# A pooling mixer and gated ConvFFN layer on one core: the second norm's factors by DMA, the first averaging matrices by GpSimd's queue, another order of the first loads

## The chip, the cores and the metric

The kernel runs on one core of one Trainium2 chip. The metric is device time in microseconds (us) of one execution. Before the change, three runs gave 671.47, 671.95 and 671.97 us.

The engines named below are TensorE (PE in the profile; PEld is its weight load), VectorE (DVE), ScalarE (ACT), GpSimd (POOL) and SyncE (SP). SP and POOL each issue DMAs on a queue of their own (q1 and q0 in the profile); 16 DMA engines carry them out.

## The reference

x is 1024 tokens by 1024 channels, float32. With these sizes there is one layer, and its mixer is the pooling one:

```python
def rms_norm(x, g):
    y = x * lax.rsqrt(jnp.mean(x * x, axis=-1, keepdims=True) + EPS)
    return y * g

def pool_mixer(x, w, b, scale):        # windows 2, 4, 8, 16: one for each 256 channels
    ...
    groups.append(window_sum / count - xf[..., group])
    ...
    y = jnp.einsum('bsgc,gcd->bsgd', d, w).reshape(bsz, seq, D_MODEL) + b
    return scale * y

def conv_ffn(x, w_in, conv_w, conv_b, w_out):
    h = causal_depthwise_conv(x @ w_in, conv_w, conv_b)
    val, gate = jnp.split(h, 2, axis=-1)
    return (jax.nn.silu(gate) * val) @ w_out

h = rms_norm(x, norm_mix_g)
x = x + pool_mixer(h, pool_w, pool_b, pool_scale)
x = x + conv_ffn(rms_norm(x, norm_ffn_g), ffn_w_in, ffn_conv_w, ffn_conv_b, ffn_w_out)
```

The hidden width of the ConvFFN is 2 x 2816.

## The kernel before

**Stages.** x is cut into 8 tiles of 128 tokens. The mixer handles a tile at a time; its results, normed a second time and transposed, fill the operand n2f. Then come the product with w_in (1024 x 5632), the convolution and gate, and the product with w_out (2816 x 1024), both as seven products of half-size blocks in place of eight, in float32r parts (rows L402 and L761 of the profile). These two matrix stages take up nearly all of the span. The change touches the mixer only, which is the first 65 us.

**The mixer for tile j.** `rstd_of` (ScalarE squares a tile with a sum along its rows, takes a root; VectorE makes of it two factors whose product is 1/sqrt) gives the row factors. `mixer_norm` multiplies the averaging matrices (`band`, for tile 0 `band0`, which is a part of the constants `cst`) by them, so the norm is folded into the matrices. `windows` multiplies x by these matrices on TensorE (psd); tile 0's first columns are corrected with `fac`, the later tiles' first 16 tokens with `edges`, which come from the last 16 tokens of all tiles (`x_edge`, `edge_norm`, `mixer_edges`, ps_edges). ScalarE copies psd to dh. `mixer_out` multiplies dh by the scaled weights wps, adds the bias through the rows `bias_hl` and a matrix of ones (psy, L288 and L291), and VectorE adds x (x1). `mixer_out_stats` takes the statistics of x1 by `rstd_of`, `ffn_norm` makes n2 from x1, the row factor and `gains[0]`, the second norm's factors with one row in each of the 128 partitions, and `ffn_operand` transposes it (pst).

**Factors before.** `gain_rows` makes that tile of factors: the factors stand in `par_sb`, 8 to a partition (columns from GF); eight products on TensorE with `ident`, each with one column broadcast, spread them over all partitions, and ScalarE copies the result to `gain_b`, times FOLD (64). FOLD is a constant that is also in the averaging matrices.

**Order.** Each engine works its instructions in order. `issue_after` sets an instruction behind another on the same engine; the last part of the code shown lists the order of the mixer's first tiles by such marks. SP's queue is issued in this order: x0 in two halves; cst up to E0 (band0 and fac); x1; 16 columns of par_sb (from GM: first and second norm's factors); the rest of cst; pool_w in two; x2; x_edge; then, behind the bias rows, x3 to x7 and the convolution's factors in par_sb. POOL's queue loads only rows8 here (pool_scale and pool_b, in 8 partitions). POOL itself fills `idle`, `pick`, `bias_hl` and the four matrices of `band`. TensorE first multiplies `idle` seven times (`keep_warm`), then spreads pool_scale with `pick` (ps_scale).

**PSUM.** The mixer's banks (`bank2`) rotate over three double banks: idle_ps, psd0, ps_gain, psd1, psy0 and so on.

Of the kernel before, what the change touches and what calls it, by code (L numbers as in the profile page):

```python
# [7 lines left out]
F32 = mybir.dt.float32  # L8
F32R = mybir.dt.float32r
BF16 = mybir.dt.bfloat16  # L10
AF = mybir.ActivationFunctionType
ALU = mybir.AluOpType
PSUM = bass.MemoryType.PSUM

P = 128
S = 1024
D = 1024
F = 2816
NS = S // P
NK = D // P  # L20
NF = F // P
NG = 4
# [3 lines left out]
EPS = 1e-6  # L26

FOLD = 2 * D**0.5

CW, CB, GM = 0, 3 * 2 * NF, 4 * 2 * NF  # L30
GF = GM + NK
NPAR = GF + NK


FAC = NG * P // 2
E0 = FAC + 2 * NG * HALO
# [27 lines left out]
def trunk_kernel(ctx: ExitStack, tc: tile.TileContext, x, consts, par, rows, pool_w, w_in, w_out, out):  # L64
    nc = tc.nc

    const = ctx.enter_context(tc.tile_pool(name="const", bufs=1))
    dram = ctx.enter_context(tc.tile_pool(name="dram", bufs=1, space=bass.MemoryType.DRAM))
# [8 lines left out]
    pp = pre.enter_context(tc.tile_pool(name="pre", bufs=1))  # L77
    ps_p = pre.enter_context(tc.tile_pool(name="ps_p", bufs=3, space=PSUM))

    def bank2(name):  # L80
        return ps_p.tile([P, 2 * NH], F32, tag="ps", name=name)

    def raw_tile(name):
        return work.tile([P, 2, D], F32, tag="raw", name=name, bufs=2)
# [15 lines left out]
    def load_x(j):  # L100
        if j < 2 or j >= 2 + XBUFS:
            xs[j] = hls.tile([P, D], F32, tag="hl", name=f"x{j}", bufs=7)
        else:
            xs[j] = pp.tile([P, D], F32, tag="x", name=f"x{j}", bufs=XBUFS)
        for cols in HALVES if j == 0 else [slice(0, D)]:
            nc.sync.dma_start(xs[j][:, cols], x[j * P : (j + 1) * P, cols])

    cst = pp.tile([P, BD], F32, tag="cst", name="cst")
# [3 lines left out]
    def affine(t, src, op, fill, base, pattern, step):  # L112
        nc.gpsimd.affine_select(out=t, in_=src, compare_op=op, fill=fill, base=base, pattern=pattern, channel_multiplier=step)

    rows_raw = raw_tile("rows_raw")
    scale = rows_raw[:, 0, :GRP]
    rows8, bias8 = (rows_raw[:NK, 1, i * NH : i * NH + 2 * P].rearrange("k (r p) -> k r p", p=P) for i in range(2))
    bias8 = bias8.bitcast(F32R)
    idle = work.tile([P, NH], BF16, tag="sum", name="idle", bufs=3)
    nc.gpsimd.memset(idle, 0.0)  # L120
    nc.vector.memset(scale, 0.0)
    eps_t = const.tile([P, 1], F32, tag="eps", name="eps_t")
    nc.vector.memset(eps_t, D * EPS)
    warm = pp.tile([P, 1], F32, tag="warm", name="warm")
    with tc.issue_after(nc.scalar.dma_start(scale[:NG, :], rows[0].rearrange("(g d) -> g d", d=GRP)).ins):
        nc.scalar.activation(warm, eps_t, AF.Sqrt)

    nc.gpsimd.dma_start(rows8, rows.rearrange("r (k p) -> k r p", p=P))

    pick = pp.tile([P, NG], F32, tag="pick", name="pick")  # L130
    nc.gpsimd.memset(pick, 0.0)
    affine(pick, pick, ALU.not_equal, 1.0, 0, [[1, NG]], -1)
    bias_hl = pp.tile([P, D], F32R, tag="bias_hl", name="bias_hl")
    nc.gpsimd.memset(bias_hl.bitcast(F32), 0.0)
    for g, w in enumerate(WINDOWS):

        m = band[:, g, :]
        nc.gpsimd.memset(m, FOLD / w)
        affine(m, m, ALU.is_ge, 0.0, 0, [[1, P]], -1)
        affine(m, m, ALU.is_gt, 0.0, w, [[-1, P]], 1)  # L140
        affine(m, m, ALU.not_equal, FOLD / w - FOLD, 0, [[1, P]], -1)
    par_sb = const.tile([P, NPAR + PAD], F32, tag="par", name="par_sb")
    wp_raw = raw_tile("wp_raw").rearrange("p a (c d) -> p (a c) d", d=GRP)

# [5 lines left out]

    keep_warm(7)
    load_x(0)
    nc.sync.dma_start(cst[:, :E0], consts[:, :E0])
    load_x(1)
    nc.sync.dma_start(par_sb[:, GM:NPAR], par[:, GM:])
    nc.sync.dma_start(cst[:, E0:], consts[:, E0:])
    for g in range(0, NG, 2):
        nc.sync.dma_start(wp_raw[:, 2 * g : 2 * g + 4, :], pool_w[g : g + 2].rearrange("g (k p) d -> p (g k) d", p=P))
    load_x(2)
# [6 lines left out]
    ident = cst[:, ID:]  # L166

    marks = {}

    def rstd_of(src, name, halves=False):  # L170
        junk = pp.tile([P, D], BF16, tag="junk", name=f"junk_{name}")
        st = pp.tile([P, 8], F32, tag="st", name=f"st_{name}", bufs=8)
        part, first, ms, root, q, inv, half = (st[:, i : i + 1] for i in range(7))
        bias = eps_t
        if halves:
            bias = first
            nc.scalar.activation(junk[:, :NH], src[:, :NH], AF.Square, accum_out=half)
            nc.vector.tensor_scalar(first, half, D * EPS, None, op0=ALU.add)
            src, junk = src[:, NH:], junk[:, NH:]
        nc.scalar.activation(junk, src, AF.Square, accum_out=part)  # L180
        marks[name] = nc.scalar.activation(root, part, AF.Sqrt, bias=bias).ins
        nc.vector.tensor_scalar(ms, part, first if halves else D * EPS, None, op0=ALU.add)

        nc.vector.scalar_tensor_tensor(q, root, root, ms, op0=ALU.mult, op1=ALU.add)
        nc.vector.reciprocal(inv, q)
        return root, inv
# [6 lines left out]
    def edge_norm():  # L193
        marks["edge"] = normed(edge_band, band_e, rstd_of(x_edge, "e"))

    def mixer_norm(j):
        t = bands[j] = pp.tile([P, NG, P], F32, tag="bandr", name=f"bandr{j}", bufs=2)
        for groups in [slice(0, 2), slice(2, 4)] if j == 0 else [slice(0, NG)]:
            marks[f"band{j}"] = normed(t[:, groups, :], (band if j else band0)[:, groups, :], stats[j])
# [18 lines left out]
    wps = pp.tile([P, 2 * NG, GRP], F32, tag="wps", name="wps")  # L218
# [8 lines left out]
    def mixer_weights(scale_b, chunks):  # L227
        for c in chunks:
            marks["wps"] = nc.vector.scalar_tensor_tensor(
                wps[:, c, :], scale_b[c // 2], par_sb[:, GM + c : GM + c + 1], wp_raw[:, c, :], op0=ALU.mult, op1=ALU.mult  # L230
            ).ins
# [4 lines left out]
    def pool_bias():  # L236
        marks["bias"] = nc.scalar.activation(bias8[:, 0, :], b8, AF.Copy).ins
        marks["bias_dve"] = nc.vector.tensor_tensor(bias8[:, 1, :], b8, bias8[:, 0, :].bitcast(F32), ALU.subtract).ins
        for l in range(2):
            m = nc.sync.dma_start(bias_hl[l : l + 1, :].bitcast(F32), bias8[:, l, :].bitcast(F32)).ins  # L240
        with tc.issue_after(m):
            for j in range(3, NS):
                load_x(j)
            nc.sync.dma_start(par_sb[:, :GM], par[:, :GM])

    def gain_rows():
        ps = bank2("ps_gain")
        for k in range(NK):
            gain = par_sb[:, GF + k : GF + k + 1].to_broadcast([P, P])
            marks["gain_pe"] = nc.tensor.matmul(ps[:, k * P : (k + 1) * P], gain, ident, start=True, stop=True).ins  # L250
        gain_b = pp.tile([P, D], F32, tag="gain_b", name="gain_b")
        marks["gain"] = nc.scalar.activation(
            gain_b.rearrange("p (k s a) -> p k a s", k=NK, a=2), ps.rearrange("p (k a s) -> p k a s", k=NK, a=2), AF.Copy, scale=FOLD
        ).ins
        return gain_b

    ds, gains = {}, []

    def window_sums(j):
        ps = bank2(f"psd{j}")  # L260
# [19 lines left out]
    n2s = {}  # L280
# [16 lines left out]
            mixer_out_stats(j)  # L297

    def mixer_out_stats(j):
        n2s[j] = (n2s[j], rstd_of(n2s[j], f"b{j}"))  # L300

    def ffn_norm(j):
        x1, r = n2s[j]
# [179 lines left out]
    def stat(j):  # L483
        if j in xs and j not in stats:
            stats[j] = rstd_of(xs[j], f"a{j}", halves=j == 0)
# [13 lines left out]
    with tc.issue_after(marks["dh0"]), tc.issue_after(marks["wps"]):  # L499
        pool_bias()  # L500
    with tc.issue_after(marks["bias_dve"]):
        mixer_weights(scale_b, range(1, 2 * NG))
    with tc.issue_after(marks["psd0"]), tc.issue_after(marks["bias"]):
        gains.append(gain_rows())
    with tc.issue_after(marks["gain"]), tc.issue_after(marks["wps"]):
        stat(2)
        mixer_norm(2)
    with tc.issue_after(marks["gain_pe"]), tc.issue_after(marks["a2"]):
        mixer_window(1)
    with tc.issue_after(marks["dh1"]), tc.issue_after(marks["band2"]):  # L510
        edge_norm()
# [11 lines left out]
    with tc.issue_after(marks["dh1+"]), tc.issue_after(marks["edges"]):  # L523
        mixer_out_stats(0)
# [37 lines left out]
    halves = [slice(0, 2), slice(2, 4)]  # L562
# [28 lines left out]
    def take(name):  # L591
# [15 lines left out]
    src = {  # L607
        "A11": lambda f: g_dram[f][:, s0], "A21": lambda f: g_dram[f][:, s1],
        "A12": lambda f: g_dram[f + NP2][:, s0], "A22": lambda f: g_dram[f + NP2][:, s1],
        "B11": lambda f: w_out[f * P : (f + 1) * P, s0], "B12": lambda f: w_out[f * P : (f + 1) * P, s1],  # L610
        "B21": lambda f: w_out[(f + NP2) * P : (f + NP2 + 1) * P, s0],
        "B22": lambda f: w_out[(f + NP2) * P : (f + NP2 + 1) * P, s1],
    }
# [91 lines left out]
    for k in range(-SLOOK, len(oevents)):  # L705
        p, f = oevents[k + SLOOK] if k + SLOOK < len(oevents) else (None, 0)
# [8 lines left out]
        with tc.issue_after(lasts[-1]) if lasts else nullcontext():  # L715
# [12 lines left out]
            p, f = oevents[k]  # L728
# [9 lines left out]
        if f == 0 and opens:  # L738
            for i in range(4):
                tag = ("XXYY" if set_ == "X" else "YZZZ")[i]  # L740
# [15 lines left out]
        for i, g, c, bank in steps:  # L756
            a, b = oops[p, g]
            alone = opens and (p, i) != ("P4", 3)
            for m, (u, v) in enumerate(((0, 0), (0, 1), (1, 0))):
                first = g == (NP2 - TAIL if c.start else 0) and m == 0  # L760
                nc.tensor.matmul(  # L761
                    bank, a[:, u, i * P : (i + 1) * P], woven(b[:, v, :])[:, c.start // 2 : c.stop // 2, :],
                    start=opens and first, stop=g == NP2 - 1 and m == 2, skip_group_check=not alone,
# [83 lines left out]
```

## Time and profile before

| | us |
|---|---|
| median of three runs | 671.95 |
| the profiled execution | 671.79 |
| its span, first to last instruction | 670.1 |
| TensorE busy | 663.4 |
| VectorE busy | 568.6 |
| ScalarE busy | 339.4 |
| GpSimd busy | 47.6 |

The mean granted clock of TensorE is 0.999. Durations and places below are those of the profiled execution; a time in us counts from its first instruction. In the chain of waits a row is: start, length, what the end of the kernel waited for there. In the timeline a row is: start, busy time, engine, line, operation, output <- inputs, shape, count, and in brackets the idle time just before it with what ended it. "issue" is time with no wait that the profile shows. A table by stretch has the busy time of each engine with its count of instructions, then the granted clock, the mean busy share of the 16 DMA engines (it can pass 1, as packets overlap) and GB/s. A DMA queue's row has packets, MB and the time that its packets took as a share of 16 engines; an issue's row has its size and the us from issue to landing.

### The profile page before, as it was taken

Reading aid. Unit: us, or ns where it says so; the run is one execution under the profiler, and the core shown is the slowest. Engines: PE = TensorE matmul, PEld = TensorE weight load, DVE = VectorE, ACT = ScalarE, POOL = GpSimd, SP = SyncE. Lnnn points to the kernel's source line nnn. Section 1 sums busy time; section 2 is a strip of 40 time slices with the busy share of each in tenths; the row PEclk is TensorE's granted clock in tenths of the full one; section 3 lists DMA queues with packets and bytes.
Section 4 is the critical chain, followed back from the end, with each engine's and each line's share of the span. In section 5 each row is a group of like instructions: output and inputs, shape, how many; then the busy total and the mean of one; then the engine's idle time right before and its main releaser. Section 6 shows DMA issues by size and latency. Waiting matters only on the chain.

```text
span 670.1 us, 8721 instructions
## 1 busy us (share of the span) xinstructions
PE 663.4 (99%) x3164; PEld 578.8 (86%) x3164; DVE 568.6 (85%) x841; ACT 339.4 (51%) x517; POOL 47.6 (7%) x73
## 2 busy tenths in 40 slices
PE   9999999999999999999999999999999999999997
PEld 7899788888888888888888888888888888888886
DVE  4697999998888888888888887887987988999995
ACT  5696655555445544444544544554554444444441
POOL 3021020110011111111011101100000000000000
PEclk9999999999999999999999999999999999999999
DMA  8884353544444444444443444429999810122241
GB/s 267 293 227 112 107 127 126 173 139 115 141 119 111 132 142 141 143 128 126 140 141 127 111 141 119 119 95 343 340 332 339 295 46 0 63 94 81 63 125 64
DMA packets 41603, 101.23 MB, mean 151 GB/s; under 512 B 4668, under 2 KB 6616, under 8 KB 38744
## 3 DMA queue, kind: packets, MB, share of 16 engines
q1 hardware_dynamic: 34608, 88.07, 37.3%
q0 software_dynamic: 6944, 12.59, 11.4%
q8 instruction: 25, 0.41, 0.3%
q14 instruction: 18, 0.15, 0.1%
q10 hardware_dynamic: 8, 0.00, 0.0%
HBM read 68.14 MB, written 19.92 MB: 131 GB/s over the span
## 4 chain that ended last, share of the span: by engine, by line
PE 79%; DVE 14%; ACT 3%; DMA 1%; issue 1%; SPq 1%; ACTq 0%; DVEq 0%
PE Y L402 24%; PE oP L761 17%; PE X L402 16%; PE Z L402 15%; PE psy L288 4%; DVE oAP L92 3%; DVE oBP L92 3%; ACT oAP L91 2%; DMA x<-in_x_dram 1%; PE psd L203 1%; DVE T L341 1%; DVE z L355 1%; DVE blk L352 1%; DVE A12s L352 1%; DVE B21s L352 1%
## 5 line engine op out<-in xcount | busy, mean ns | idle before, releaser
L761 PE MATMUL oP<-oBP,oAP 128*128 128x512 f32 (+1 forms) x924 | 198.9, 378 | 0.3 <-DVE oBP L92 0.3
L761 PEld LDWEIGHTS oP<-oBP,oAP 128*128 128x128 f32 x924 | 174.0, 189 | 25.3 <-DVE oBP L92 0.7
L402 PE MATMUL X<-B,A11s 128*128 128x512 f32 x264 | 61.5, 380 | 0.2 <-DVE A11s L92 0.2
L402 PE MATMUL Z<-T,S1s 128*128 128x512 f32 x264 | 60.9, 380 | 0.6 <-DVE T L341 0.3
L402 PE MATMUL Y<-T,S3s 128*128 128x512 f32 x264 | 60.7, 379 | 0.2 <-DVE q L431 0.2
L402 PE MATMUL Y<-T,A22s 128*128 128x512 f32 x264 | 60.8, 380 | 0.0
L402 PE MATMUL Y<-T,S2s 128*128 128x512 f32 x264 | 60.7, 379 | 0.0
L402 PE MATMUL X<-B,A12s 128*128 128x512 f32 x264 | 60.7, 379 | 0.0
L402 PE MATMUL Z<-B,S4s 128*128 128x512 f32 x264 | 60.5, 379 | 0.0
L402 PEld LDWEIGHTS Z<-T,S1s 128*128 128x128 f32 x264 | 49.7, 189 | 8.4 <-ACT T L340 0.7
L402 PEld LDWEIGHTS Y<-T,S3s 128*128 128x128 f32 x264 | 49.8, 189 | 7.6 <-DVE q L431 0.6
L402 PEld LDWEIGHTS Y<-T,A22s 128*128 128x128 f32 x264 | 49.7, 189 | 7.7 <-DVE hb L439 0.6
L402 PEld LDWEIGHTS X<-B,A11s 128*128 128x128 f32 x264 | 49.7, 189 | 7.6 <-DVE A11s L92 0.6
L402 PEld LDWEIGHTS Z<-B,S4s 128*128 128x128 f32 x264 | 49.8, 189 | 7.3 <-DVE r L436 0.3
L402 PEld LDWEIGHTS Y<-T,S2s 128*128 128x128 f32 x264 | 49.9, 189 | 7.1
L402 PEld LDWEIGHTS X<-B,A12s 128*128 128x128 f32 x264 | 49.8, 189 | 7.0
L91 ACT ACTIVATE oBP<-blk 128x512 fp32r<-128x512 f32 x53 | 33.1, 625 | 44.2 <-PE oP L761 30.6
L460 ACT ACTIVATE gate<-gate 128x1024 f32<-128x1024 f32 x22 | 23.3, 1057 | 47.4 <-DVE gate L451 47.4
L91 ACT ACTIVATE oAP<-blk 128x512 fp32r<-128x512 f32 x55 | 34.1, 620 | 19.6 <-DVE blk L352 17.0
L92 DVE TENSOR_TENSOR oBP<-blk,oBP 128x512 fp32r<-128x512 f32 x53 | 36.5, 689 | 8.6 <-ACT oBP L91 6.6
L92 DVE TENSOR_TENSOR oAP<-blk,oAP 128x512 fp32r<-128x512 f32 x55 | 37.8, 687 | 2.9 <-ACT oAP L91 2.9
L450 DVE SCALAR_TENSOR_TENSOR val<-ha,par_sb,val 128x1023 f32<-128x1023 f32 x22 | 28.2, 1283 | 13.6 <-ACT val L449 13.6
(131 smaller groups left out, 958.1 us busy)
## 6 DMA issues: line engine op xcount, KB each, us to landing
win<-in_w_in_dram SPq DMA_DIRECT2D x22, 1024.0 KB, 4.8
g_dram<-val SPq DMA_DIRECT2D x22, 512.0 KB, 2.7
blk<-g_dram SPq DMA_DIRECT2D x33, 256.0 KB, 5.2
blk<-in_w_out_dram SPq DMA_DIRECT2D x31, 256.0 KB, 5.7
win<-win POOLq DMA_DIRECT2D x26, 256.0 KB, 3.5
S<-in_w_in_dram SPq DMA_DIRECT2D x22, 256.0 KB, 3.5
S<-win POOLq DMA_DIRECT2D x22, 256.0 KB, 4.2
A12s<-g_dram SPq DMA_DIRECT2D x22, 256.0 KB, 5.3
```

The costliest lines, as they stand in the source:

```text
L91: nc.scalar.activation(t[:, 0, :], src, AF.Copy)
L92: m = nc.vector.tensor_tensor(t[:, 1, :], src, t[:, 0, :].bitcast(F32), ALU.subtract)
L203: m = nc.tensor.matmul(ps[:, c * P : (c + 1) * P], src[:, c * P : (c + 1) * P], weights[:, c // 2, :], start=True, stop=True)
L288: nc.tensor.matmul(o, dh[:, c, :], wps[:, c, :], start=c % 4 == 0, stop=False, skip_group_check=True)
L341: nc.vector.tensor_tensor(l, src, h.bitcast(F32), ALU.subtract)
L352: nc.vector.tensor_tensor(out, a, b, ALU.subtract)
L355: nc.vector.tensor_tensor(out, a, b, ALU.add)
L402: nc.tensor.matmul(bank, a[:, i, ks], woven(b[:, l, k, :]), start=opens and m == 0, stop=m == 11, skip_group_check=not opens)
L450: nc.vector.scalar_tensor_tensor(t[:, 1:], src[:, : S - 1], w[1], t[:, 1:], op0=ALU.mult, op1=ALU.add)
L460: nc.scalar.activation(gate, gate, AF.Silu)
L761: nc.tensor.matmul(bank, a[:, u, i * P : (i + 1) * P], woven(b[:, v, :])[:, c.start // 2 : c.stop // 2, :], start=opens and first, stop=g ...
```

## The change

- `pick` is made first on POOL; then POOL's queue loads band0 (cst up to FAC). `idle` is filled by VectorE. `bias_hl` is filled behind the band matrices.
- `gain_row`, a row of 1024 factors in DRAM, is written by POOL's queue from par. SP loads it into all partitions as `gain_b`, between x4 and x5.
- SP issues x1 right behind x0; then the rest of cst (fac, edge matrices, ident), and 8 columns of par in place of 16.
- The eight products and the copy of `gain_rows` are gone, and a PSUM bank with them. FOLD moves into `rstd_of` for the second norm: a scale on the root, a multiplication beside the addition on VectorE, a bias `eps_f`.

```diff
-    nc.gpsimd.memset(idle, 0.0)
+    pick = pp.tile([P, NG], F32, tag="pick", name="pick")
+    nc.gpsimd.memset(pick, 0.0)
+    affine(pick, pick, ALU.not_equal, 1.0, 0, [[1, NG]], -1)
+    nc.gpsimd.dma_start(cst[:, :FAC], consts[:, :FAC])
+    nc.vector.memset(idle, 0.0)
     nc.vector.memset(scale, 0.0)
...
+    eps_f = const.tile([P, 1], F32, tag="eps_f", name="eps_f")
+    nc.vector.memset(eps_f, D * EPS / FOLD**2)
...
-    pick = pp.tile([P, NG], F32, tag="pick", name="pick")
-    nc.gpsimd.memset(pick, 0.0)
-    affine(pick, pick, ALU.not_equal, 1.0, 0, [[1, NG]], -1)
-    bias_hl = pp.tile([P, D], F32R, tag="bias_hl", name="bias_hl")
-    nc.gpsimd.memset(bias_hl.bitcast(F32), 0.0)
     for g, w in enumerate(WINDOWS):
...
+    bias_hl = pp.tile([P, D], F32R, tag="bias_hl", name="bias_hl")
+    nc.gpsimd.memset(bias_hl.bitcast(F32), 0.0)
+    gain_row = dram.tile([1, D], F32, tag="gain_row", name="gain_row")
+    nc.gpsimd.dma_start(gain_row.rearrange("o (k p) -> p (o k)", p=P), par[:, GF:])
...
     load_x(0)
-    nc.sync.dma_start(cst[:, :E0], consts[:, :E0])
     load_x(1)
-    nc.sync.dma_start(par_sb[:, GM:NPAR], par[:, GM:])
-    nc.sync.dma_start(cst[:, E0:], consts[:, E0:])
+    nc.sync.dma_start(cst[:, FAC:], consts[:, FAC:])
+    nc.sync.dma_start(par_sb[:, GM:GF], par[:, GM:GF])
...
-    def rstd_of(src, name, halves=False):
+    def rstd_of(src, name, halves=False, fold=1.0):
...
-        bias = eps_t
+        bias = eps_t if fold == 1.0 else eps_f
...
-        marks[name] = nc.scalar.activation(root, part, AF.Sqrt, bias=bias).ins
-        nc.vector.tensor_scalar(ms, part, first if halves else D * EPS, None, op0=ALU.add)
+        marks[name] = nc.scalar.activation(root, part, AF.Sqrt, bias=bias, scale=fold**-2).ins
+        if fold == 1.0:
+            nc.vector.tensor_scalar(ms, part, first if halves else D * EPS, None, op0=ALU.add)
+        else:
+            nc.vector.tensor_scalar(ms, part, D * EPS, fold**-2, op0=ALU.add, op1=ALU.mult)
...
             for j in range(3, NS):
                 load_x(j)
+                if j == 4:
+                    gain_rows()
...
     def gain_rows():
-        ps = bank2("ps_gain")
-        for k in range(NK):
-            gain = par_sb[:, GF + k : GF + k + 1].to_broadcast([P, P])
-            marks["gain_pe"] = nc.tensor.matmul(ps[:, k * P : (k + 1) * P], gain, ident, start=True, stop=True).ins
         gain_b = pp.tile([P, D], F32, tag="gain_b", name="gain_b")
-        marks["gain"] = nc.scalar.activation(
-            gain_b.rearrange("p (k s a) -> p k a s", k=NK, a=2), ps.rearrange("p (k a s) -> p k a s", k=NK, a=2), AF.Copy, scale=FOLD
-        ).ins
-        return gain_b
-
-    ds, gains = {}, []
+        nc.sync.dma_start(gain_b, gain_row.to_broadcast([P, D]))
+        gains.append(gain_b)
...
-        n2s[j] = (n2s[j], rstd_of(n2s[j], f"b{j}"))
+        n2s[j] = (n2s[j], rstd_of(n2s[j], f"b{j}", fold=FOLD))
...
-    with tc.issue_after(marks["psd0"]), tc.issue_after(marks["bias"]):
-        gains.append(gain_rows())
-    with tc.issue_after(marks["gain"]), tc.issue_after(marks["wps"]):
+    with tc.issue_after(marks["bias"]), tc.issue_after(marks["wps"]):
         stat(2)
         mixer_norm(2)
-    with tc.issue_after(marks["gain_pe"]), tc.issue_after(marks["a2"]):
+    with tc.issue_after(marks["psd0"]), tc.issue_after(marks["a2"]):
         mixer_window(1)
```

More of the change, by code (lines that the diff above doesn't have):

```diff
@@ L243, in pool_bias @@
                 load_x(j)
+                if j == 4:
+                    gain_rows()
             nc.sync.dma_start(par_sb[:, :GM], par[:, :GM])
+    gains = []
     def gain_rows():
-        ps = bank2("ps_gain")
-        for k in range(NK):
-            gain = par_sb[:, GF + k : GF + k + 1].to_broadcast([P, P])
-            marks["gain_pe"] = nc.tensor.matmul(ps[:, k * P : (k + 1) * P], gain, ident, start=True, stop=True).ins
         gain_b = pp.tile([P, D], F32, tag="gain_b", name="gain_b")
-        marks["gain"] = nc.scalar.activation(
-            gain_b.rearrange("p (k s a) -> p k a s", k=NK, a=2), ps.rearrange("p (k a s) -> p k a s", k=NK, a=2), AF.Copy, scale=FOLD
-        ).ins
-        return gain_b
-    ds, gains = {}, []
+        nc.sync.dma_start(gain_b, gain_row.to_broadcast([P, D]))
+        gains.append(gain_b)
+    ds = {}
     def window_sums(j):
```

## The prediction

> **What bounds the kernel now.** I read the page first, for its chain; then the chain of waits of the first 110 us; then the timeline around the places the change touches; last the DMA view and the busy times by stretch.
>
> ```profile
> PE 79%; DVE 14%; ACT 3%; DMA 1%; issue 1%; SPq 1%; ACTq 0%; DVEq 0%
> ```
>
> TensorE is the end of most of the span, and nothing in the change touches the products of the two large matrix stages. So the only question is when those products can begin, and the chain in order of time says what sets that:
>
> ```profile
> 4.66 9.38 DMA x<-in_x_dram
> 14.04 0.02 issue
> 14.06 1.16 ACT junk_a L180 x2
> ...
> 15.54 0.91 ACT dh L273
> 16.45 1.04 ACT junk_e L180 x2
> ...
> 17.82 1.05 ACT junk_a L180 x2
> 18.86 0.09 issue
> 18.95 2.04 PE ps_edges L203 x16
> ...
> 23.27 3.46 PE psy L288 x16
> ...
> 95.76 0.92 PE X L402 x3
> ```
>
> The load of x2 (the third tile of x) is issued at 4.66 and lands at 14.04. ScalarE, which works in order, then does x2's squares, the copy dh1, the squares of the edge rows and those of x3; at 18.95 TensorE starts ps_edges, and from 23.27 to 95.76 follow the tiles of the mixer and a stretch of VectorE, each released by the one before. I therefore carry a delay or gain of x2's landing, of ps_edges' start, one for one to the end. The profiled execution took 671.79 us (span 670.1 and 1.69 around it); the three runs shown have a median of 671.95, 0.16 above it. All sums below go from 671.79.
>
> **What is beside the chain.** The timeline of the first 31 us:
>
> ```profile
> 0.93 0.27 DVE L121 MEMSET rows_raw<- 128x256 f32 x1 [0.93 <-PEq L838]
> 1.19 0.17 DVE L207 MEMSET ones<- 128x128 f32 x1
> 1.48 0.75 POOL L128 DMA_DIRECT2D rows_raw<-in_rows_dram  x1 [0.15 <-issue]
> 4.35 3.15 PE L224 MATMUL ps_scale<-rows_raw,pick 128*128 128x256 f32 x8
> 5.46 1.52 POOL L113 TENSOR_SCALAR_AFFINE_SELECT band<-band 128x128 f32<-128x128 f32 x6
> 6.65 0.79 DVE L189 TENSOR_SCALAR bandr<-cst,st_a 128x256 f32<-128x256 bf16 x2 [0.99 <-DMA cst<-in_consts_dram]
> 7.34 1.95 PE L203 MATMUL psd<-bandr,x 128*128 128x128 f32 x16
> 9.12 1.95 PE L250 MATMUL ps_gain<-cst,par_sb 128*128 128x128 f32 x16
> 11.11 1.12 ACT L252 ACTIVATE gain_b<-ps_gain 128x1024 f32<-128x1024 f32 x1
> 11.29 1.54 SPq L240 DMA_DIRECT2D bias_hl<-rows_raw  x2
> 12.88 2.44 SPq L106 DMA_DIRECT2D x<-in_x_dram  x5
> 14.06 1.06 ACT L180 ACTIVATE junk_a<-x 128x1024 bf16<-128x1024 f32 x1 [1.84 <-DMA x<-in_x_dram]
> 16.19 0.71 PE L291 MATMUL psy<-bias_hl,ones 128*128 128x512 f32 x2
> 16.74 1.96 PE L203 MATMUL psd<-bandr,x 128*128 128x128 f32 x16
> 25.22 1.28 DVE L306 SCALAR_TENSOR_TENSOR n<-x,st_b,gain_b 128x1024 f32<-128x1024 f32 x1
> 29.77 0.89 POOL L363 DMA_DIRECT2D S<-win  x1 [22.79 <-DMA S<-in_w_in_dram]
> 29.87 1.04 ACT L180 ACTIVATE junk_a<-x 128x1024 bf16<-128x1024 f32 x1
> ```
>
> Read the row of 14.06: ScalarE stood idle 1.84 us for x2. Whatever the change saves ScalarE before 14.06 only makes that wait longer.
>
> **Part 1, the factors leave PE and ACT.** Removed are the 16 passes of ps_gain, 1.95 us of TensorE, and the eviction, 1.12 us of ScalarE: 3.07 us of work. ScalarE's 1.12 joins the 1.84 of waiting: 0. TensorE's 1.95 lets the products of tile 0 come earlier, but the next thing that matters there, psd2 at 16.74, needs x2's statistics: 0. The bounds are 0 and, should TensorE and not ScalarE hold ps_edges back, the time from psd2's end (16.74 + 1.96 = 18.70) to 18.95: -0.25. I take 0, as psd2 can't start before x2 lands. The factor FOLD goes into a Sqrt's scale and a second operation of one VectorE instruction: as many instructions as before, 0.
>
> **Part 2, averaging matrices by POOL's queue, idle's memset on DVE.** VectorE waited 0.99 us for cst at 6.65. But psd0, which needs the result, follows ps_scale on TensorE, which runs to 4.35 + 3.15 = 7.50; psd0 starts as that ends. So the wait going brings psd0 nothing: 0. If the matrices come late, psd0, dh0 and the bias follow one for one; the cover is ScalarE's 1.84 + 1.12 = 2.96 us. On POOL an issue costs 0.75; rows8 stands behind it, and the band selections, done at 6.98, lose the bias_hl memset from ahead of them, so band is ready in time for its use near 9.9. The memset of idle takes, by the two rows 0.27 for 256 and 0.17 for 128 columns, about 0.47 for 512 on VectorE: done at 1.4, about as before; the memset of rows_raw behind it, and the load, the table and the first squares behind that on ScalarE, come some 0.45 later, still within psd0's cover. The sum of part 2 is 0, with the same 2.96 as cover.
>
> **Part 3, SP's order.** One issue fewer stands ahead of x2 (0.43 and a 0.04 gap). Whether x2 lands 0.47 earlier depends on the queue:
>
> ```profile
> 4.00:8.00 4.00, 4.00 (x16) 3.29 (x15) 1.74 (x7) 1.34 (x6) 2.98 (x13) 1.00 0.94 287
> 8.00:12.00 4.00, 4.00 (x38) 4.00 (x37) 2.35 (x9) 3.29 (x6) 0.00 (x0) 1.00 1.10 370
> 12.00:14.00 2.00, 2.00 (x15) 1.84 (x14) 2.00 (x6) 0.23 (x1) 0.00 (x0) 1.00 0.79 164
> ```
>
> The last two columns are the DMA engines' share and GB/s: 0.94 and 1.10 from 4 to 12 us. x2 waits for bytes ahead of it, and those are the same bytes (cst's two pieces are cut elsewhere, one by POOL). I take 0; the bounds are -0.47 and 0.
>
> **Part 4, the row of factors.** This is what is new. Its first DMA writes par's 128 x 8 factors into a row with neighbours of one partition 512 bytes apart, so 1024 separate words, 64 for each of 16 engines. The trace before has no such write. Small packets it has:
>
> ```profile
> q0 software_dynamic: 4, 0.00, 2.2%
> q0 software_dynamic: 32, 0.01, 0.5%
> q0 software_dynamic: 137, 0.26, 70.3%
> q1 hardware_dynamic: 174, 1.07, 99.8%
> x_edge<-in_x_dram SPq DMA_DIRECT2D x1, 512.0 KB, 9.9
> ```
>
> The first is POOL's queue from 3.95 to 4.05 us, four packets under 512 bytes: 2.2% of 16 x 0.1 us is 0.035 us, 9 ns each. The second is the same queue from 0 to 8 us, 24 such and eight of 1 KB: 0.64 us, so (0.64 - 0.22) / 8 = 53 ns for a packet of 1 KB. The third, 34 to 36 us, is 22.5 us for 137 packets, mostly of 2 KB: 164 ns. So 64 words cost an engine between 64 x 9 ns = 0.6 us and 64 x 164 ns = 10.5 us; I take 0.6, the row nearest in size. The Trainium skill, DMA: Bandwidth & Descriptors, section Rules for kernel authors, speaks against this edit: a non-contiguous last dimension becomes one descriptor per element, and should be rearranged. By it the count is 1024 and the sum as here; were eight factors one packet, 8 x 9 ns would be lost and the time 671.8. No run so far shows which.
>
> Where do these 0.6 us fall? POOL is done with bands and bias_hl near 7.6 (6.98, less 0.98 and 0.53 of memsets moved, plus the new issue of some 0.9, plus 0.98 again). Its earlier DMA, issued at 29.77, shows how such a transfer stands beside queue 1: from 30 to 34 us the fourth row shows queue 1 alone at 99.8%, and POOL's packets come from 34 on. It waits until a transfer in progress is through. So I put the words behind x2 and ahead of x_edge and the bias rows. x_edge lands at 5.74 + 9.9 = 15.64 and is first read near 16.45: 0.8 of room, enough for 0.6. The bias rows are queued behind x_edge and are read at 16.19; 0.6 later, less the 0.25 between psd2's end and ps_edges, leaves **+0.35**.
>
> The second DMA, the row to all partitions, is SP's, between x4 and x5. It waits for the first; behind it on SP are x5 to x7, the convolution's factors, the stores of x1 and the first loads of w_in. SP gets there near 13.9 and waits perhaps 1 us. The row then lands as other 512 KB loads do, by about 20; it is used at 25.22, 5 us later. x5 is used at 29.87. The loads of w_in move by one transfer of 0.52 MB at 370 GB/s, 1.4 us, and with them the sum at 29.77; its successors have waits of their own. All 0; beyond 25.2 us the norm, and VectorE behind it, would slip one for one.
>
> **The sum** is 0 + 0 + 0 + 0.35: 671.79 + 0.35 = about 672.1.
>
> **The rivals.**
> (a) The words get in ahead of x2. Then x2 itself is 0.6 later with no room: 672.4. For it speaks that POOL's transfer can be ready by about 10 us, when x2's packets only begin. The Trainium skill, same page, section Queues, rings and completion order, would have the engines take turns between queues packet by packet, which mixes the words among x2's packets; the row of 30 to 34 us shows no such turns.
> (b) The loads come sooner. From 4 to 8 us they ran at 287 GB/s, from 8 to 12 at 370, and cst's pieces lie in the first stretch. If the new cut removes that loss, (370 - 287) x 4 / 370 = 0.9 us is won for x2, x_edge and bias alike: 670.9. Against it: the same bytes are still read there.
> (c) The change does nothing: the words fall into the slack stretch of 12 to 14 us (share 0.79) and the waits removed were covered: 671.8.
> (d) Slower: a word costs as much as a packet of 1 KB, 53 ns. 64 of them hold an engine 3.4 us, x2 or the bias with it: + 3.1, 674.9. It decides from (1.34 + 0.25) / 64 = 25 ns a word on. Against it: 9 ns for the smallest packets seen; for it: those were not scattered over a row in DRAM.
>
> **The chances.** Forecast 0.40; (a) 0.15; (b) 0.20; (c) 0.10; (d) 0.15. What can be told from no change is about 0.2%, 1.34 us around 671.95. (b) passes that only if it wins more than its price: 0.06 faster. Slower are (d) and a small tail of (a): 0.17. The rest, 0.77, is within. The range goes from (b) with 0.1 to spare, 670.8, to 673.4, which is (a) with a word at 25 ns; it leaves out (d) and 0.05 of tails.
>
> **What would show it.** In the profile after: ScalarE's wait for x2 should end between 14.0 and 14.7 and be about 3 us long; POOL's queue should show some 1000 tiny packets between 9 and 16 us, and their share gives the price of a word; the bias product should start near 16.5 and ps_edges near 19.3; the norm near 25.5 must not wait for a DMA. If x2's squares start before 13.5, (b) is right; if after 15.4, (d). I'd be wrong altogether if the order on SP or POOL came out other than written, so that x5 or w_in's loads stood behind a late row, or if a shift in the first 20 us were swallowed in the stretch of VectorE before 95.76.

## The result and the profile after

| | us |
|---|---|
| before, median of 4 runs of this comparison | 671.71 |
| changed, median of 4 runs (676.39 to 678.71) | 677.64 |
| changed, the profiled execution | 678.71 |
| its span | 677.0 |

The ratio is 1.0088, with a 95% interval of 1.0075 to 1.0100: 5.9 us slower, outside the range of 670.8 to 673.4. The profiled execution is the slowest of the four, 6.9 us above that of before, and its chain accounts for these 6.9.

The chain of waits of the changed kernel from 8 us on (start, length, what the end waited for):

```profile
12.35 8.62 DMA bias_hl<-rows_raw
20.98 0.14 issue
21.11 1.19 PE psy L296 x2
22.31 3.41 PE psd L210 x16
25.72 2.59 PE ps_edges L210 x16
28.31 1.79 PE psd L210 x16
30.09 3.46 PE psy L293 x16
```

The last row is the 23.27 of before: 6.82 us later, and from there to the end nothing more is lost. The two bias rows, 4 KB each, take 8.62 us. The timeline shows what else waited:

```profile
6.85 1.05 DVE L196 TENSOR_SCALAR bandr<-cst,st_a 128x256 f32<-128x256 bf16 x2 [0.81 <-DMA cst<-in_consts_dram]
7.38 0.98 POOL L146 DMA_DIRECT2D gain_row<-in_par_dram  x1
17.72 1.06 ACT L184 ACTIVATE junk_a<-x 128x1024 bf16<-128x1024 f32 x1 [6.34 <-DMA x<-in_x_dram]
20.44 0.33 SPq L259 DMA_DIRECT2D gain_b<-gain_row  x1
21.11 1.19 PE L296 MATMUL psy<-bias_hl,ones 128*128 128x512 f32 x2 [4.96 <-DMA bias_hl<-rows_raw]
22.11 3.62 PE L210 MATMUL psd<-bandr,x 128*128 128x128 f32 x16
32.51 1.28 DVE L311 SCALAR_TENSOR_TENSOR n<-x,st_b,gain_b 128x1024 f32<-128x1024 f32 x1
```

x2 comes 3.7 us later than before (17.72 against 14.06), the bias 4.9 later (21.11 against 16.19). SP issues gain_b at 20.44: until then it waits for gain_row, which POOL issued at 7.38. The norm at 32.51 waits for no DMA. Also psd2's 16 passes take 3.62 us, not 1.96.

The table by stretch of the changed kernel, its last three columns being granted clock, DMA share and GB/s:

```profile
12.00:16.00 4.00, 4.00 (x23) 3.38 (x21) 2.44 (x7) 0.00 (x0) 0.00 (x0) 1.00 0.81 98
16.00:21.00 5.00, 0.15 (x1) 0.00 (x0) 1.08 (x4) 2.72 (x5) 0.00 (x0) 0.94 0.38 52
21.00:28.00 7.00, 6.89 (x33) 6.72 (x34) 3.30 (x9) 2.52 (x6) 0.00 (x0) 0.55 0.93 317
```

and the same stretches before:

```profile
12.00:16.00 4.00, 4.00 (x24) 3.55 (x22) 2.80 (x9) 2.13 (x5) 0.00 (x0) 1.00 0.90 253
16.00:21.00 5.00, 4.72 (x36) 4.02 (x34) 3.60 (x10) 3.12 (x7) 0.00 (x0) 1.00 0.93 358
21.00:28.00 7.00, 6.75 (x39) 6.18 (x40) 4.05 (x13) 5.51 (x9) 0.00 (x0) 1.00 0.82 300
```

From 12 to 21 us the DMA engines move 98 and then 52 GB/s where they had moved 253 and 358. From 21 to 28 us TensorE's granted clock is 0.55 where it had been 1.00. The DMA view of the changed kernel says what was going on, and what it doesn't show:

```profile
q1 hardware_dynamic: 1284, 2.14, 73.1%
q0 software_dynamic: 32, 0.00, 0.7%
x<-in_x_dram SPq DMA_DIRECT2D x3, 512.0 KB, 11.0
gain_row<-in_par_dram POOLq DMA_DIRECT2D x1, 4.0 KB, 13.0
```

These are the rows of 8 to 21 us. A transfer of 4 KB took 13.0 us to land, yet its queue is put down for 32 packets and 0.7%. These packets lie between 12 and 15 us; the row landed at 20.4. The price isn't in the packets of POOL's queue. It shows in SP's queue, which from 14 to 20 us moves 0.26 MB, in 102 packets and 45% of the engines' time: some 0.42 us for each packet, where the kernel before has some 0.11 from 8 to 21 us (1777 packets, 97.1%), and gaps between them.

### The profile page after: what moved, and what is told of

Read it like the earlier page. It is cut to its first block, busy times and chain, and to the rows that moved or that the text cites. A ratio compares the mean times of both kernels' runs of the same rounds, so it can differ in the third digit from the quotient of the medians.

```text
span 677.0 us, 8693 instructions
## 1 busy us (share of the span) xinstructions
PE 664.8 (98%) x3148; PEld 579.7 (86%) x3148; DVE 569.3 (84%) x843; ACT 338.3 (50%) x516; POOL 47.8 (7%) x74
## 4 chain that ended last, share of the span: by engine, by line
PE 79%; DVE 15%; ACT 2%; DMA 2%; issue 1%; SPq 0%; ACTq 0%; DVEq 0%
PE Y L407 24%; PE oP L764 16%; PE X L407 16%; PE Z L407 15%; PE psy L293 4%; DVE oAP L92 3%; DVE oBP L92 3%; ACT oAP L91 2%; PE psd L210 2%; DVE T L346 1%; DMA bias_hl<-rows_raw 1%; DVE z L360 1%; DVE blk L357 1%; DVE A12s L357 1%; DVE B21s L357 1%
```

## The experiments

Theory 1: the 1024 words written one by one hold up the DMA engines, and with them x2, x_edge and the bias. Theory 2: the new cut and order of the loads delays x2. Theory 3: SP's wait for the row costs. Ratios are to runs of the kernel before on the same chip, with 95% intervals; the medians come from several chips, so it is the ratios that should be set side by side.

**The row as an input.** Against the changed kernel:

```diff
-    nc.gpsimd.dma_start(rows8, rows.rearrange("r (k p) -> k r p", p=P))
+    nc.gpsimd.dma_start(rows8, rows[:2].rearrange("r (k p) -> k r p", p=P))
...
-    gain_row = dram.tile([1, D], F32, tag="gain_row", name="gain_row")
-    nc.gpsimd.dma_start(gain_row.rearrange("o (k p) -> p (o k)", p=P), par[:, GF:])
...
-        nc.sync.dma_start(gain_b, gain_row.to_broadcast([P, D]))
+        nc.sync.dma_start(gain_b, rows[2:3].to_broadcast([P, D]))
...
-        "rows": _np.stack([a["pool_scale"][0], a["pool_b"][0]]),
+        "rows": _np.stack([a["pool_scale"][0], a["pool_b"][0], a["norm_ffn_g"][0]]),
```

> The changed kernel, with the factors as a third row of the input rows: gain_b is loaded straight from it, and the write of 1024 words and SP's wait for it are gone; all else of the change stays. Theory 1 (the words written one by one hold up the DMA engines, and so x2, x_edge and the bias): x2's squares start near 14.0, 671.7 us within 0.8. Theory 2 (the cut of cst, POOL's load or the order of SP's loads delays x2): x2's squares still start after 17, 675 us or more.

672.29 us, ratio 1.0011 (1.0002 to 1.0021). Most of the loss of 5.9 goes with the write and the wait; about 1 us over the kernel before is left. x2's squares start at 15.15, which is 1.1 later than before and not near the 14.0 that I expected.

**The words alone.** The two lines of gain_row's write added to the kernel before; nothing reads it.

> The kernel before, with nothing added but the write of the 1024 words into a row of DRAM that nobody reads, at the same place on POOL. Theory 1: x2's squares start near 17.5, the bias lands near 20, 676 to 679 us. Theory 2: 671.7 us. Theory 3 (SP's wait for the row is what costs): nobody waits for the row here, so 671.7 to 672.4 us.

677.21 us, ratio 1.0087 (1.0071 to 1.0102): the whole loss, with nobody waiting for the row. Theories 2 and 3 can't give that. In the timeline:

```profile
17.32 1.06 ACT L182 ACTIVATE junk_a<-x 128x1024 bf16<-128x1024 f32 x1 [4.99 <-DMA x<-in_x_dram]
18.56 0.69 PE L293 MATMUL psy<-bias_hl,ones 128*128 128x512 f32 x2 [2.13 <-DMA bias_hl<-rows_raw]
```

x2 is about as late as in the changed kernel (17.32 against 17.72). The bias landed near 18.5, 1.5 earlier than I expected; in this execution the chain goes through x2.

**Runs of 8.** The changed kernel, with the row in order of partition:

```diff
-    nc.gpsimd.dma_start(gain_row.rearrange("o (k p) -> p (o k)", p=P), par[:, GF:])
+    nc.gpsimd.dma_start(gain_row.rearrange("o (p k) -> p (o k)", p=P), par[:, GF:])
...
-        nc.vector.scalar_tensor_tensor(n2, x1, r[1], gains[0], op0=ALU.mult, op1=ALU.mult)
+        by_k = lambda t: t.rearrange("q (k p) -> q k p", p=P)
+        nc.vector.scalar_tensor_tensor(by_k(n2), by_k(x1), r[1], gains[0].rearrange("q (p k) -> q k p", p=P), op0=ALU.mult, op1=ALU.mult)
```

> The changed kernel, with the row in DRAM ordered by partition, so that its write is 128 runs of 32 bytes in place of 1024 of 4; VectorE reads gain_b with a step of 8 words. Theory 1, the price going by the number of writes: an eighth of some 7 us of held up engines, x2 late by under 1 us, 671.7 to 672.8 us. Theory 1, the price going by bytes or by any small write to that row: as the changed kernel, near 677. Should the step cost VectorE time, the norm's rows show more than 1.28 us.

675.89 us, ratio 1.0064 (1.0048 to 1.0081), near neither number, and the two halves of the edit have to be read apart. The write became cheap: SP issues gain_b at 14.39 without standing still, the row landed 6.8 us after its issue, and x2 came at 14.72; ps_edges started at 19.61, where the loads alone (below) have 19.55. What is lost beyond that is lost behind ps_edges, and it is VectorE's. The view of the tile gain_b, here and before:

```profile
L312 DVE SCALAR_TENSOR_TENSOR n<-x,st_b,gain_b x8: 2073/2134/2183, 25.9 to 73.9; 128x1024 f32<-128x1024 f32 x8
```
```profile
L306 DVE SCALAR_TENSOR_TENSOR n<-x,st_b,gain_b x8: 1282/1285/1285, 25.2 to 70.6; 128x1024 f32<-128x1024 f32 x8
```

A step of 8 words makes each of the eight norms 0.85 us longer, and in this kernel's chain the norms then alternate with VectorE's sums and ScalarE's statistics, in place of TensorE alone.

**The loads alone.** The kernel before with parts 2 and 3 of the change:

```diff
-    nc.gpsimd.memset(idle, 0.0)
...
+    nc.gpsimd.dma_start(cst[:, :FAC], consts[:, :FAC])
+    nc.vector.memset(idle, 0.0)
...
-    nc.sync.dma_start(cst[:, :E0], consts[:, :E0])
     load_x(1)
+    nc.sync.dma_start(cst[:, FAC:], consts[:, FAC:])
     nc.sync.dma_start(par_sb[:, GM:NPAR], par[:, GM:])
-    nc.sync.dma_start(cst[:, E0:], consts[:, E0:])
```

> The kernel before, with the change's loads and nothing else of it: pick first, averaging matrices of tile 0 by POOL's queue, idle by VectorE, x1 right behind x0, then the rest of cst; the factors still by TensorE and ScalarE. If the loads of the change cost nothing: 671.3 us within 0.5. If the 1.0 us that the row as an input stood above the kernel before comes from the loads: 672.3 us, with the first norm's matrices or x1 later than before.

672.26 us, ratio 1.0011 (1.0002 to 1.0019): the same ratio as with the row as an input. The loads by themselves cost 0.8 us. Two rows of it:

```profile
cst<-in_consts_dram POOLq DMA_DIRECT2D x1, 128.0 KB, 5.9
7.41 0.74 DVE L189 TENSOR_SCALAR bandr<-cst,st_a 128x256 f32<-128x256 bf16 x2 [1.15 <-DMA cst<-in_consts_dram]
```

Issued by POOL, the averaging matrices come 5.9 us after the issue, and VectorE starts at 7.41 where it started at 6.65. x2's squares start at 14.66, 0.6 later than before. By which of the loads x2 is late wasn't tried.

**What about a word costs.** Six kernels add only a write that nobody reads to the kernel before, at the place of gain_row's, and vary it (the line that makes its target is left out here):

```diff
 half:    + nc.gpsimd.dma_start(gain_row[:, : D // 2].rearrange("o (k p) -> p (o k)", p=P), par[:, GF : GF + NK // 2])
 apart:   + nc.gpsimd.dma_start(gain_row.rearrange("o (k p s) -> p (o k) s", p=P, s=16)[:, :, 0], par[:, GF:])   # s = 4 and 2 too
 SBUF:    + nc.gpsimd.dma_start(words[:, :, 0], par[:, GF:])                                # words: [P, NK, 2]
 ordered: + nc.gpsimd.dma_start(gain_row.rearrange("o (p k) -> p (o k)", p=P), par[:, : 22 * NK : 22])
```

> The kernel before, with only the write of words added, 512 of them (4 columns of factors) in place of 1024; nobody reads them. If the price goes by the number of words: half the loss of the 1024 alone (5.9 us), 674.2 us within 0.7. If it is one price for any such transfer: 677 us.

> The kernel before, with the 1024 words written one by one into every other word of a tile in SBUF in place of a row in DRAM; nobody reads them. If the number of separate words costs whatever the target: 677 us. If writing single words to DRAM is what costs: 671.3 to 672.3 us (64 words an engine at 9 ns are 0.6 us).

> The kernel before, with the 1024 words written into DRAM 64 bytes apart, over 64 KB in place of 4 KB; nobody reads them. If the words cost because neighbours of one stretch of DRAM are written by many engines at once: well under 677, near 672 to 674 us. If each single word costs by itself: 677 us, or more.

> The kernel before, with the 1024 words written into DRAM 16 bytes apart, over 16 KB; nobody reads them. So far: 1024 words 4 bytes apart cost 5.9 us, 512 words 4 bytes apart 6.5, 1024 words 64 bytes apart 0.2. If the words that share a stretch of 64 bytes are written one after the other, there are 4 of them here in place of 16: a quarter, 1.5 us, part of it within the room of x_edge and the bias, 671.5 to 673.0 us, the words landed some 9 us after their issue. If any sharing costs the whole: 677 us.

> The kernel before, with the 1024 words written into DRAM 8 bytes apart; nobody reads them. A stretch of 64 bytes then takes 8 words, all from one engine's 8 partitions; 4 bytes apart it takes 16, from two engines. If it matters that two engines share the stretch: 671.3 to 672.6 us, the words landed within 8 us of their issue. If the spacing alone decides: some loss, 673 to 677 us.

> The kernel before, with 1024 words read 88 bytes apart (columns of the convolution's factors) and written in order of partition, so that they lie 4 bytes apart but 64 neighbours come from one engine, one after the other; nobody reads them. If sharing between engines is what costs: 671.3 to 672.6 us. If words 4 bytes apart cost by themselves: 676 to 678 us. Where the engine writes its 8 words of a partition as one run, this is the run of 32 bytes again, and tells only that the reads cost nothing.

| written, by 4 bytes | bytes from word to word | us to landing | median us | ratio |
|---|---|---|---|---|
| 1024, DRAM (e2) | 4 | 12.7 | 677.21 | 1.0087 (1.0071 to 1.0102) |
| 512, DRAM (e6) | 4 | 11.8 | 677.93 | 1.0096 (1.0083 to 1.0110) |
| 1024, DRAM (e11) | 8 | 9.0 | 672.52 | 1.0020 (1.0011 to 1.0030) |
| 1024, DRAM (e9) | 16 | 7.7 | 672.55 | 1.0012 (1.0003 to 1.0021) |
| 1024, DRAM (e8) | 64 | 8.3 | 671.68 | 1.0003 (0.9994 to 1.0013) |
| 1024, DRAM, ordered (e12) | 4 | 16.1 | 681.28 | 1.0144 (1.0128 to 1.0160) |
| 1024, SBUF (e7) | 8 | 7.5 | 672.34 | 1.0014 (1.0004 to 1.0023) |

The number of words isn't the price: half of them cost as much, and as many cost under 2 us once they lie 8 bytes apart. It is the spacing. The stretch written grows with the spacing, from 4 to 64 KB, but a short stretch is not dear by itself: the runs of 8 fill the same 4 KB. At 8 bytes something is left: x2's squares start at 15.90 in the profiled execution, 1.8 later than before. Whether the target matters isn't shown: the words in SBUF lay 8 bytes apart, and cost about what 8 bytes apart cost in DRAM. From 8 to 21 us, the write with 64 bytes from word to word has this DMA view:

```profile
q1 hardware_dynamic: 1737, 4.07, 98.1%
q0 software_dynamic: 32, 0.00, 0.7%
```

POOL's queue has the same row as in the changed kernel; SP's moves 4.07 MB where it moved 2.14 there.

The ordered write is the dearest, with 10.2 us, more than I had expected either way. If each DMA engine takes eight partitions in order, as I assumed and no view shows, 64 neighbours come there from one engine, one right after the other, and that two engines share a stretch of 64 bytes wouldn't be needed. But this write also reads words 88 bytes apart, which no other run does by itself, so part of its price may be the reads'. I expected that a stretch shared by 4 words costs a quarter: the time at 16 bytes lies in the range that I gave, but the row lands no later than at 64 bytes, where I had expected 9 us, so a quarter isn't seen. What fits all rows is that a write close to one just made has to wait for it; that it waits the longer the sooner it follows rests on the ordered write alone. No view shows the wait itself, so this stays an inference. The table by stretch of the ordered write from 16 to 21 us:

```profile
16.00:21.00 5.00, 0.00 (x0) 0.00 (x0) 0.01 (x1) 0.00 (x0) 0.00 (x0) 0.69 0.54 22
```

Next to no work is done on any engine, and 22 GB/s move.

**The clock.** The granted clock was 0.55 from 21 to 28 us. Fillers, products that nobody reads, were to keep it up in the changed kernel, ten and then twenty:

```diff
+        if j == 0:
+            fill_ps = ps_x.tile([P, NH], F32, tag="X", name="fill_ps")
+            for _ in range(10):
+                nc.tensor.matmul(fill_ps, idle[:, :P], idle, start=True, stop=True)
         for h in range(2):
```

> The changed kernel, with ten products of idle (0.43 us each) on TensorE between tile 0's products and its bias, where it stood idle for 4.96 us. If the lower granted clock after that (psd2 took 3.62 us, ps_edges 2.80, where the kernel before shows 1.96 and 2.02) comes from TensorE's standing idle: both near 2.0 again, 2.3 to 2.5 us won, about 675.2 us. If it comes from elsewhere: 677.6 us.

678.28 us, ratio 1.0097 (1.0082 to 1.0113). A filler took 0.23 us where I had reckoned 0.43, so ten covered half the gap. The clock did stay at 1.00 and psd2 took 2.02 us; but x2's squares started at 20.55 in that execution, and ps_edges at 25.44, as in the changed kernel.

> The changed kernel once more, on one chip with the next, so that both can be set side by side: 677.6 us within 1; psd2 and ps_edges near 3.6 and 2.8 us behind TensorE's 5 us of standing idle.

678.23 us, ratio 1.0094 (1.0080 to 1.0108); x2 at 19.98.

> The changed kernel with the ten filler products, once more. The first time the granted clock stayed at 1.0 and psd2 took 2.02 us, but x2 had landed 2.8 us later than in the changed kernel's profile, and the time was no lower. If that landing was chance and the clock is on the chain: 1.5 to 2.5 us under the changed kernel. If x2 again lands later and the time is the same: the lower clock costs little, since x2, the edge rows and ScalarE's order hold ps_edges anyway.

678.76 us, ratio 1.0104 (1.0085 to 1.0124), on one chip with the run above. This time x2's squares started at 15.68, the bias came at 21.53, and the clock fell (0.50 from 21 to 24 us).

> The changed kernel with twenty filler products between tile 0's products and its bias, some 4.6 us by their 0.23 each. If the lower granted clock follows from TensorE's standing idle and is on the chain: psd2 near 2.0 us and 1.5 to 2.5 us under the changed kernel's 678.2. If the landings alone set the time: 678 us with the clock at 1.0.

678.68 us, ratio 1.0106 (1.0091 to 1.0121). The fillers ended at 20.9, and by stretch:

```profile
20.00:22.00 2.00, 1.08 (x6) 0.39 (x4) 0.15 (x1) 1.31 (x3) 0.00 (x0) 1.00 0.57 74
22.00:24.00 2.00, 1.28 (x7) 0.87 (x7) 0.93 (x3) 2.00 (x4) 0.00 (x0) 0.89 0.92 367
24.00:26.00 2.00, 2.00 (x11) 2.00 (x11) 1.43 (x6) 1.71 (x5) 0.00 (x0) 0.50 1.03 356
26.00:28.00 2.00, 2.00 (x16) 2.00 (x16) 1.86 (x4) 0.00 (x0) 0.00 (x0) 0.76 1.01 416
```

TensorE was busy 2.36 of 4 us from 20 to 24, and then, busy again, got half the clock for some 3 us. The Trainium skill, TensorE: Matmul & The Clock Gate, section Part 1: The HAM clock gate, has the clock follow TensorE's activity in windows of about 3.4 us that run on their own; a fall that comes once after 3 us of standing idle (3.21, the second run of ten fillers) and once not (3.04, the first) fits that. No filler made the kernel faster, so the clock is at most a part of the loss: in the changed kernel's profile psd2 and ps_edges together cost 2.4 us more than before, in the execution of the first filler nothing, and the times are alike. Of the eight executions of the changed kernel on record, the three with a mean granted clock of 0.997 or more took 676.39 to 677.73 us and the five with 0.994 or 0.995 took 677.45 to 678.93; later landings could be behind both. How much a kept clock would win at equal landings stays open, as the start of x2's squares lies between 15.68 and 20.66 in the profiles of the changed kernel's two runs and the three with fillers.

**Another order.** The kernel before with the row as an input, x2 between the halves of pool_w, the bias by POOL (so that x3 and x4 follow the edge rows directly):

```diff
+        if g == 0:
+            load_x(2)
-    load_x(2)
...
-            m = nc.sync.dma_start(bias_hl[l : l + 1, :].bitcast(F32), bias8[:, l, :].bitcast(F32)).ins
+            nc.gpsimd.dma_start(bias_hl[l : l + 1, :].bitcast(F32), bias8[:, l, :].bitcast(F32))
```

> The kernel before, with the factors as a third input row loaded into all partitions by SP between x4 and x5 (no products and no copy for them), x2 loaded between the two halves of pool_w, and the bias rows by POOL's queue, x3 and x4 right behind x_edge. If x2's landing is what holds the chain until the edge rows take over, and the bias rows come no later than 16: ps_edges 0.4 to 0.9 us earlier than 18.95, 670.4 to 671.1 us. If the edge rows or the bias bind at the same place: 671.4 us.

672.70 us, ratio 1.0015 (1.0007 to 1.0024), a miss. x2's squares began at 11.21, 2.85 us earlier, and it won nothing:

```profile
15.84 1.06 ACT L183 ACTIVATE junk_e<-x_edge 128x1024 bf16<-128x1024 f32 x1 [2.24 <-DMA x_edge<-in_x_dram]
18.12 0.70 PE L295 MATMUL psy<-bias_hl,ones 128*128 128x512 f32 x2 [1.76 <-DMA bias_hl<-rows_raw]
```

The edge rows and then the bias are next, and the bias, now by POOL's queue, is read at 18.12, 1.93 later than before. No version tried beats the kernel before.

## Why the prediction was wrong, point by point

- **The frame held.** What ps_edges loses is lost one for one to the end: 6.82 us at the first psy behind it, 6.9 at the end of the span.
- **Part 1, 0 for the work taken from TensorE and ScalarE: right.** The row as an input (without that work) and the loads alone (with it) have the same ratio, 1.0011.
- **Part 2, 0, and part 3, 0: off by size.** I took the wait for cst as going; it went from 0.99 to 0.81 us with the start 0.2 us later in the changed kernel, and to 1.15 with the start 0.76 later in the loads alone. Of SP's order it was right that x2 came no sooner; in the loads alone it came 0.6 later, outside my bounds of -0.47 and 0. Parts 2 and 3 together cost 0.8 us where I had 0; they weren't tried apart. This doesn't add to the price of the words: the write alone loses 5.9 us, as much as the whole change.
- **Part 4 is the step that failed:** "I take 0.6, the row nearest in size". The mechanism was the one named, words that hold the engines ahead of x_edge and the bias; the term was mis-sized. I had +0.35 for it in the sum; measured, the write alone costs 5.9 us. My sign of some 1000 tiny packets was wrong too: POOL's queue shows 32. Between my ends of 0.6 and 10.5 us I chose by size, and size wasn't what set the price: 64 bytes apart, as many words of the same size cost 0.2 us, with an interval that holds both no loss and my 0.35. Rival (d) had the doubt that the small packets seen weren't scattered over a row, at 53 ns a word and 674.9 with 0.15. Its sign, x2's squares after 15.4, came; its price was too low, and no price by the word fits, as half the words cost as much.
- **The place was partly wrong.** I put the words behind x2; x2 too was 3.7 us late. That it could be is rival (a), which had 0.6 for it.
- **The wait on SP** was reckoned at 1 us and lasted until 20.44; its cover held, as the norm at 32.51 waited for nothing.
- **Not foreseen:** the clock, which fell after TensorE had stood idle for 4.96 us.
- The two sentences that leaned on the Trainium skill, DMA: Bandwidth & Descriptors: that a last dimension out of line becomes one descriptor per element and should be rearranged (section Rules for kernel authors) was the right warning, and the runs of 8 fit it (a landing in 6.8 us in place of 13.0). It names no price: 64 bytes apart the words are as much out of line and cost 0.2 us. That queues take turns packet by packet (section Queues, rings and completion order) couldn't be settled here.

## What to carry to other kernels

A rearrangement within a small DMA to DRAM isn't small: count the separate writes and look at how close they lie, and load the data in the layout that it is needed in, or write whole runs. Price an operation that the trace lacks by its whole range until something like it, target and spacing included, has been measured. When a load on the chain is brought forward, name the next two arrivals first: here the edge rows and the bias stood right behind x2.

## What the runs showed of the hardware

- 512 or 1024 words of 4 bytes written side by side into DRAM take 11.8 to 13.0 us to land, 16.1 in order, and what the DMA engines move falls from 253 and 358 to 98 and 52 GB/s meanwhile; 16 or 64 bytes apart they land in 7.7 and 8.3 us. The Trainium skill, DMA: Bandwidth & Descriptors, section Back-pressure in remote DMA, says of transfers between cores that stalled writes stall the source engine's other queues too. Here, within one core, the table by stretch and the DMA view show SP's queue slowed, which fits; that the writes were stalled no view shows.
- The profile's packets don't show such a write: 0.7% of the engines' time, whether it takes 13.0 us and costs 5.9 or takes 8.3 and costs 0.2. The other queue does.
- VectorE's norm on 128x1024 takes 1.285 us with all operands in line and 2.134 with one input read in steps of 8 words. The Trainium skill, SBUF — State Buffer, section Door 1: The DMA port swizzle, gives lines of 16 bytes within which steps are free; 32 bytes is beyond that, and the trace agrees.
